# Modulation chunks of the attention in the rooms of x and of the early operand, on ScalarE's DMA queue

## The chip, the cores and the metric

One core of a Trainium2 chip runs the whole program. Its engines are TensorE (PE; PEld is its weight load), VectorE (DVE), ScalarE (ACT), GpSimd (POOL) and SyncE (SP), which here only issues DMAs. The metric is the device time of one execution in microseconds. The kernel before took 772.94 us as the median of three runs (772.45 to 775.13).

## The reference

A trunk of two layers on 256 tokens of width 1024, in f32. Layer 0 mixes tokens with dilated windowed attention in three groups and 16 heads, layer 1 with gated linear attention; each is followed by a gated ConvFFN. Every sub-layer reads a normed input that is scaled and shifted by a modulation vector, which comes from the condition `c`:

```python
for i in range(DEPTH):
    mod = jax.nn.silu(c) @ w_ada[i] + b_ada[i]            # 1024 x 6144 per layer
    sh1, sc1, g1, sh2, sc2, g2 = jnp.split(mod, 6, axis=-1)
    h = rmsnorm(x, norm_mix[i]) * (1.0 + sc1) + sh1
    y = dilated_mixture(h, ...) if i == 0 else gla_mixer(h, ...)
    x = x + g1 * y
    h = rmsnorm(x, norm_ffn[i]) * (1.0 + sc2) + sh2
    x = x + g2 * conv_ffn(h, ...)
return rmsnorm(x, norm_final)
```

`dilated_mixture` computes for each head and group `softmax(q k^T + bias) v` within a causal window, mixes the three groups by their log sums, and multiplies by `w_out`.

## The kernel before

Everything is kept transposed, channels on the 128 partitions and the 256 tokens along the row. A product in f32 is made of three passes with split operands, hi times hi, lo times hi and hi times lo (`mm3`, L197 to L199). So each weight tile goes through three steps, in `split`: SP loads it into a buffer `raw` (1 MB for 2048 columns, L181), ACT casts it to `whi` in two halves (L187), and DVE subtracts to get `wlo` in two halves (L191). There are four `raw` buffers and three pairs of whi and wlo.

The modulation is computed beside the rest, in 48 chunks of 1 MB. `ada_chunk(l, n)` (L151) loads a chunk of `w_ada` with SP into **one of the same four `raw` buffers** (L155), and makes with DVE two products with a sum along the row (L160, into `dot`), each turned by ACT into a column of `mod` (L168, L170). Eight chunks are done in the opening. The other 40 stand in the list `rest`, and `next_ada` takes the next one wherever it is called. 18 of them fall into the attention.

The attention goes through the 16 heads in eight pairs. The turn u of the loop computes for pair u the q and k of three groups (`queries`, each with one wqk tile of 2048 columns: 48 matmuls), then v (`values`, two wv tiles of 1536 columns, into pv[0] and pv[1]), then the scores, and the outputs of the pair before: `turn` transposes the normed probabilities `pn` into `t` (L520), ACT copies `t` to `pt` (L521), `outputs` multiplies `pt` with `v` into `po` (L528, L532) and ACT and DVE make ohi and olo of it (L537, L538). `evacuate` copies q with ACT and k with DVE out of the accumulators (L548, L549), and `by_group` copies v with ACT (L563 to L566). `maxima` and `probabilities` add the bias, take the maximum on DVE (L489), the exponential on ACT (L502) and scale on DVE (L508, L509). Pair 7's outputs are computed between the matmuls of the projection (`project`, accumulators `py`), which follows the attention.

`x_all` holds x. At first it holds it with its tokens in the order of their residues, which the attention's norm reads in the opening. In the turn u = 2, SP loads x in its own order into it (L692), for the residual behind the attention (L327). `early_x` are eight tiles of 272 columns that hold an operand of the ConvFFN's first products; column 256 of each takes a shift (`shift_columns`, L286), the others a scaled x (L292).

The order of the instructions on each engine is set by a scheduler that simulates a time line, under the constraints that `behind(...)` and `issue_after` set. Each engine works through its own list in order, SP's DMA issues too: what stands behind a waiting instruction waits as well.

Of the kernel before, what the change touches and what calls it, by code (L numbers as in the profile page):

```python
# [11 lines left out]
F32 = mybir.dt.float32  # L12
# [6 lines left out]
P = 128  # L19
D = 1024  # L20
T = 256
KT = D // P
# [35 lines left out]
def trunk(ctx: ExitStack, tc: tile.TileContext, I, out):  # L58
    nc = tc.nc
# [3 lines left out]
    state = ctx.enter_context(tc.tile_pool(name="state", bufs=1))  # L63
# [8 lines left out]
    def bank(name="ps", tag=None):  # L72
        tag = tag or next(cycle)
        return psum.tile([P, 512], F32, tag=tag, name=name, bufs={"p": 2, "s": 4, "t": 2}[tag])
# [11 lines left out]
    x_all = state.tile([P, KT, T], F32, name="x_all")  # L86
# [12 lines left out]
    def col(at):  # L99
        return small[:, at : at + 1]  # L100
# [19 lines left out]
    @contextmanager  # L120
    def behind(*those):

        with ExitStack() as st:
            for i in those:
                st.enter_context(tc.issue_after(i.ins))
            yield
# [24 lines left out]
    def ada_chunk(l, n, dmas=1):  # L151
        raw = wraw.tile([P, 2048], F32, tag="raw", name="ada_raw")
        for i in range(dmas):
            c = slice(2048 * i // dmas, 2048 * (i + 1) // dmas)
            nc.sync.dma_start(raw[:, c], I["w_ada"][l, n][:, c])  # L155
        for s in range(2):
            piece, kt = ADA_ORDER[2 * n + s]
            dot = tmp.tile([P, 1], F32, tag="dot", name="dot", bufs=4)
            w = raw[:, D * s : D * s + D]
            last_dot[0] = nc.vector.tensor_tensor_reduce(  # L160
                w, w, c_bc, op0=ALU.mult, op1=ALU.add, scale=1.0, scalar=0.0, accum_out=dot,
            )
            m = state.tile([P, 1], F32, tag=f"mod{l}{piece}{kt}", name="mod")
            b = col(C_BADA + 48 * l + 8 * piece + kt)
            if piece in (1, 4):
                g = col((C_NMIX if piece == 1 else C_NFFN) + 8 * l + kt)
                b1 = (16 if piece == 4 else 0) + 8 * l + kt
                last = nc.scalar.activation(m, dot, AF.Identity, scale=g, bias=one_b[:, b1 : b1 + 1])  # L168
            else:
                last = nc.scalar.activation(m, dot, AF.Identity, bias=b)  # L170
            mod[l, piece, kt] = m
        return last


    last_load, copied, last_lo = [None], [None], [None]
# [101 lines left out]
        chain[kt] = chain[7] = i, j  # L277
        return h_hi[kt], h_lo[kt]

    early_x = [state.tile([P, T + 16], F32, tag=f"ex{k}", name="early_x") for k in range(KT)]  # L280
    last_x, last_sum = [None, None], []

    def shift_columns(l, sub):
# [97 lines left out]
    on_act = [norm_ops[1]]  # L381
# [71 lines left out]
    rest = [(0, n) for n in range(8, 24)] + [(1, n) for n in range(24)]  # L453

    def next_ada():
        if rest:
            ada_chunk(*rest.pop(0))


    heads = [slice(E * hh, E * hh + E) for hh in range(2)]  # L460

    def scores(q, k):
# [52 lines left out]
    def turn(tiles, normed_p, pt):  # L515
        for i in tiles:
            t = bank("t", "ttss"[i])
            for j in range(3):
                c = slice(P * j, P * j + P)
                last = nc.tensor.transpose(t[:, c], normed_p[i][:, c], ident)  # L520
            pt_copy[0] = nc.scalar.copy(pt[:, i, :], t[:, 0:KEYS])  # L521
        return last
# [20 lines left out]
    def evacuate(q, k, g, pq, pk):  # L543

        if g:
            i = nc.scalar.mul(q[g], pq, 0.125)  # L548
            return i, nc.vector.tensor_copy(k[g], pk)  # L549
        qh, ql = q[0]  # L550
        pk = in_order(pk)
        kh, kl = (as_tokens(z[:, 0:T]) for z in k[0])
        nc.scalar.mul(qh, pq, 0.125)
        i = nc.scalar.copy(kh, pk)
        nc.vector.scalar_tensor_tensor(ql, pq, 0.125, qh.bitcast(F32), op0=ALU.mult, op1=ALU.subtract)
        return i, nc.vector.tensor_tensor(kl, pk, kh.bitcast(F32), op=ALU.subtract)
# [11 lines left out]
    def new_qk():  # L568
        q = [[att.tile([P, T], F32R, tag=f"q0{i}", name="q") for i in range(2)]]
        k = [[att.tile([P, T + 2], F32R, tag=f"k0{i}", name="k") for i in range(2)]]  # L570
        for z in k[0]:
            nc.gpsimd.memset(z[:, T:].bitcast(F32), 0.0)
        for g in (1, 2):
            q.append(att.tile([P, T], F32, tag=f"q{g}", name="q"))
            k.append(att.tile([P, T], F32, tag=f"k{g}", name="k"))
        return q, k

    def values(u, half, pv, after=(), low=()):
        with behind(*chain[7]):
            w = split(I["wv"][u - 1, half], 1536, after=(after, after), low=low, late=low)  # L580
        for k4 in range(4):
            kt = 4 * half + k4
            wv = parts(w, 384 * k4, 384)
            for t in range(2):
                ht = [y[:, P * t : P * t + P] for y in h[kt]]
                end = mm3(pv[t][:, :384], ht, wv, kt == 0, kt == KT - 1)
        return end

    def queries(u, g, *qk):
        pq, pk, middle, end = raw_queries(u, g, after=pt_copy[:1] if (u, g) == (3, 0) else ())  # L590
        kept[:] = evacuate(*qk, g, pq, pk)
        with behind(kept[1]):
            next_ada()
        return middle, end

    def raw_queries(u, g, tag="p", low=(), by_parts=False, after=()):
        w = split(I["wqk"][u - 2, g], 2048, low=low, late=low, after=(after, after))
        pqk = bank("pqk", tag)
        pq, pk = pqk[:, :T], pqk[:, T:]
        if by_parts:  # L600
            for part in range(3):
                for kt in range(KT):
                    for i, ps in enumerate((pq, pk)):
                        at = 2 * P * kt + P * i
                        end = mm(ps, w[part == 2][:, at : at + P], h[kt][part == 1], start=(part == kt == i == 0),
                                 stop=(part == 2 and kt == KT - 1 and i == 1))
            return pq, pk, None, end
        for kt in range(KT):
            s, e = kt == 0, kt == KT - 1
            mm3(pq, parts(w, 2 * P * kt), h[kt], s, False)  # L610
            end = mm3(pk, parts(w, 2 * P * kt + P), h[kt], False, e)
            if kt == 3:
                middle = end
        return pq, pk, middle, end

    def by_groups(pv):
        v = [att.tile([P, NG * P], F32, tag=f"v{t}", name="v") for t in range(2)]
        for n in range(2):
            by_group(v[n], pv[n])
        return v  # L620

    def bias_of(u):
        with tc.issue_after(last_load[0].ins):
            return load_bias(u)
# [45 lines left out]
        values(1, 0, pv, low=left[-1][1:])  # L670
    end = values(1, 1, pv, after=left[-1][:1], low=evacuated[1:])
    with behind(evacuated[1]):
        next_ada()
    v = by_groups(pv)
    before = probabilities(*maxima(s, bias))
    bias1 = bias_of(1)
# [4 lines left out]
    for u in range(2, NPAIR):  # L681
        if u > 2:
            bias = bias_of(u)
            qk = new_qk()
        with behind(last):
            if u > 2:
                queries(u, 0, *qk)
            middle, end = queries(u, 1, *qk)
        if u == 2:
            bias = bias_of(u)  # L690
            with tc.issue_after(last_load[0].ins):
                nc.sync.dma_start(x_all, I["xT"])  # L692
        with behind(middle):
            turn((0, 1), *before)
        with behind(end):
            turned = turn((2, 3), *before)
        first = pt_copy[:1] if u == 2 else ()
        if u == 2:
            turned_pt, before = before[1], probabilities(*raised)
        middle, end = queries(u, 2, *qk)  # L700
        if u == 2:
            with behind(end):
                outputs(0, v0, turned_pt)
                turn((0, 1), *before)
        second = pt_copy[:1] if u == 2 else ()
        pv = [bank("pv", "p") for _ in range(2)]
        end = values(u, 0, pv, after=first)
        if u == 2:
            with behind(end):
                turned = turn((2, 3), *before)  # L710
        if u < NPAIR - 1:
            end = values(u, 1, pv, after=second)
        with behind(end, turned):
            s, last = scores(*qk)
        with behind(last):
            last = outputs(u - 1, v, before[1])
        if u == NPAIR - 1:
            with behind(last):
                values(u, 1, pv, low=kept[1:])
        v = by_groups(pv)  # L720
        before = probabilities(*maxima(s, bias))
# [222 lines left out]
    for n in range(4):  # L944
# [7 lines left out]
        for i in range(2):  # L952
            kt = 2 * n + i
# [146 lines left out]
    for n in range(4):  # L1100
# [7 lines left out]
        for et in range(2):  # L1108
            i = 2 * n + et
# [156 lines left out]
```

## Time and profile before

| what | us |
|---|---|
| median of three runs | 772.94 |
| the profiled execution | 769.98 |
| its span in the profile | 768.2 |
| opening, to the first q copied by ACT | 58.1 |
| attention, turns u = 2 to 7, to the last po | 267 |

The granted clock of TensorE was 0.999 in the mean. A row of the timeline has the start, the duration, the engine, the line and the operation; in brackets is the idle time of the engine just before it, and what ended it. A row with x3 stands for several equal instructions in a row. Matmuls overlap: one that is shown with 0.28 us is followed by the next after 0.11. "q1 hardware_dynamic" in the page's list of queues is what SP and ACT issue; over the span the DMA engines were busy with it for 67.4%:

```profile
q1 hardware_dynamic: 36032, 184.84, 67.4%
HBM read 184.17 MB, written 1.10 MB: 241 GB/s over the span
```

### The profile page before, as it was taken

Reading aid. Unit: us, or ns where it says so; the run is one execution under the profiler, and the core shown is the slowest. Engines: PE = TensorE matmul, PEld = TensorE weight load, DVE = VectorE, ACT = ScalarE, POOL = GpSimd, SP = SyncE. Lnnn points to the kernel's source line nnn. Section 1 sums busy time; section 2 is a strip of 40 time slices with the busy share of each in tenths; the row PEclk is TensorE's granted clock in tenths of the full one; section 3 lists DMA queues with packets and bytes.
Section 4 is the critical chain, followed back from the end, with each engine's and each line's share of the span. In section 5 each row is a group of like instructions: output and inputs, shape, how many; then the busy total and the mean of one; then the engine's idle time right before and its main releaser. Section 6 shows DMA issues by size and latency. Waiting matters only on the chain.

```text
span 768.2 us, 15928 instructions
## 1 busy us (share of the span) xinstructions
PE 756.4 (98%) x6420; PEld 730.1 (95%) x6420; DVE 625.2 (81%) x1120; ACT 490.3 (64%) x964; POOL 12.3 (2%) x36
## 2 busy tenths in 40 slices
PE   9999999999999999999999999999999999999997
PEld 5999989999998999999999998898999999999997
DVE  6988886878878788999988868887567998899662
ACT  5566675665666578676766456736667766666552
POOL 0000000000000010000000000000010000000100
PEclk9999999999999999999999999999999999999999
DMA  9989778587787856876656976776254756565741
GB/s 346 388 307 334 255 297 292 200 331 251 276 309 253 297 200 233 279 232 230 221 184 228 334 254 241 289 274 226 79 191 165 232 207 210 177 203 206 259 153 55
DMA packets 36487, 186.29 MB, mean 243 GB/s; under 512 B 8444, under 2 KB 11004, under 8 KB 20286
## 3 DMA queue, kind: packets, MB, share of 16 engines
q1 hardware_dynamic: 36032, 184.84, 67.4%
q8 instruction: 50, 0.82, 0.4%
q10 hardware_dynamic: 382, 0.45, 0.2%
q14 instruction: 23, 0.19, 0.1%
HBM read 184.17 MB, written 1.10 MB: 241 GB/s over the span
## 4 chain that ended last, share of the span: by engine, by line
PE 68%; DMA 13%; DVE 13%; ACT 3%; issue 2%; SPq 0%; ACTq 0%; DVEq 0%
PE pab L199 10%; PE pab L197 10%; PE pab L198 10%; DMA raw<-in_wqk 6%; PE pd L197 5%; PE pd L199 5%; PE pd L198 5%; DVE wlo L191 5%; DMA ada_raw<-in_w_ada 4%; DMA raw<-in_wv 3%; DVE ada_raw L160 3%; PE py L197 2%; PE py L198 2%; PE py L199 2%; PE pv L197 2%
## 5 line engine op out<-in xcount | busy, mean ns | idle before, releaser
L191 DVE TENSOR_TENSOR wlo<-raw,whi 128x1024 fp32r<-128x1024 f32 (+2 forms) x258 | 273.3, 1093 | 60.0 <-ACT whi L187 58.9
L187 ACT CAST whi<-raw 128x1024 fp32r<-128x1024 f32 (+2 forms) x258 | 230.5, 942 | 116.3 <-PE pab L198 40.7
L199 PE MATMUL pab<-hhi,wlo 128*128 128x256 f32 x672 | 184.7, 276 | 0.0
L198 PE MATMUL pab<-hlo,whi 128*128 128x256 f32 x672 | 184.6, 276 | 0.0
L197 PE MATMUL pab<-hhi,whi 128*128 128x256 f32 x672 | 183.2, 277 | 0.0
L198 PEld LDWEIGHTS pab<-hlo,whi 128*128 128x128 f32 x672 | 126.0, 188 | 0.2
L199 PEld LDWEIGHTS pab<-hhi,wlo 128*128 128x128 f32 x672 | 126.2, 188 | 0.0
L197 PEld LDWEIGHTS pab<-hhi,whi 128*128 128x128 f32 x672 | 125.1, 188 | 0.1
L160 DVE CUSTOM_DVE_ANT_0 ada_raw<-ada_raw,c_bc 128x1024 f32<-128x1024 f32 x96 | 113.5, 1221 | 10.3 <-DMA ada_raw<-in_w_ada 10.2
L199 PE MATMUL pd<-ghi,wlo 128*128 128x256 f32 x352 | 97.1, 276 | 0.0
L198 PE MATMUL pd<-glo,whi 128*128 128x256 f32 x352 | 97.1, 276 | 0.0
L197 PE MATMUL pd<-ghi,whi 128*128 128x256 f32 x352 | 96.8, 276 | 0.0
L197 PE MATMUL pqk<-hhi,whi 128*128 128x256 f32 x328 | 92.3, 281 | 0.1
L199 PE MATMUL pqk<-hhi,wlo 128*128 128x256 f32 x328 | 91.3, 278 | 0.0
L198 PE MATMUL pqk<-hlo,whi 128*128 128x256 f32 x328 | 91.0, 277 | 0.0
L199 PEld LDWEIGHTS pd<-ghi,wlo 128*128 128x128 f32 x352 | 66.1, 188 | 0.0
L198 PEld LDWEIGHTS pd<-glo,whi 128*128 128x128 f32 x352 | 66.1, 188 | 0.0
L197 PEld LDWEIGHTS pd<-ghi,whi 128*128 128x128 f32 x352 | 65.9, 188 | 0.0
L197 PEld LDWEIGHTS pqk<-hhi,whi 128*128 128x128 f32 x328 | 61.7, 188 | 0.7 <-issue 0.3
L199 PEld LDWEIGHTS pqk<-hhi,wlo 128*128 128x128 f32 x328 | 61.7, 188 | 0.3 <-issue 0.3
L198 PEld LDWEIGHTS pqk<-hlo,whi 128*128 128x128 f32 x328 | 61.7, 188 | 0.0
L827 ACT ACTIVATE r<-pab,small 128x256 f32<-128x256 f32 x86 | 46.7, 559 | 15.5 <-DVE r L830 15.4
(226 smaller groups left out, 1385.2 us busy)
## 6 DMA issues: line engine op xcount, KB each, us to landing
ada_raw<-in_w_ada SPq DMA_DIRECT2D x46, 1024.0 KB, 5.8
raw<-in_w_up SPq DMA_DIRECT2D x42, 1024.0 KB, 4.9
raw<-in_w_down SPq DMA_DIRECT2D x32, 704.0 KB, 5.2
raw<-in_wqk SPq DMA_DIRECT2D x18, 1024.0 KB, 7.7
raw<-in_wv SPq DMA_DIRECT2D x14, 768.0 KB, 4.6
raw<-in_w SPq DMA_DIRECT2D x6, 960.0 KB, 5.8
raw<-in_w_out_a SPq DMA_DIRECT2D x4, 1024.0 KB, 7.2
raw<-in_w_v_b SPq DMA_DIRECT2D x4, 1024.0 KB, 5.0
```

Of the source, the lines that this page charges most:

```text
L160: last_dot[0] = nc.vector.tensor_tensor_reduce(w, w, c_bc, op0=ALU.mult, op1=ALU.add, scale=1.0, scalar=0.0, accum_out=dot,)
L187: copied[0] = nc.scalar.copy(hi[:, c], raw[:, c])
L191: last_lo[0] = nc.vector.tensor_tensor(lo[:, c], raw[:, c], hi[:, c].bitcast(F32), op=ALU.subtract)
L197: mm(ps, a[0], b[0], start=start, stop=False)
L198: mm(ps, a[0], b[1], start=False, stop=False)
L199: return mm(ps, a[1], b[0], start=False, stop=stop)
L827: nc.scalar.activation(r, u[:, :T], AF.Identity, scale=cw[2], bias=col(C_CB + 44 * l + f))
```

## The change

The 18 chunks of the attention no longer use `raw` and SP's queue. The eight tiles `early_x` become one tile `early_all` of 8 times 272 columns. The first 2048 columns of `early_all` and all of `x_all` are two *rooms*. `room_load(i)` loads chunk i into room i % 2, issued by ACT. The first two are issued behind ACT's last cast of the opening's weights `w0` (`on_act[0]`). `room_ada` stands where `next_ada` stood in the attention: it computes the chunk in its room, and behind it on ACT loads the chunk after the next into the same room; behind the last chunk of room 1 it loads x in its own order into `x_all`. SP's load of it in the turn u = 2 is gone. The chunks after the attention stay as they were.

```diff
@@ ada_chunk
             nc.sync.dma_start(raw[:, c], I["w_ada"][l, n][:, c])
+        return modulation(raw, l, n)
+
+    def modulation(raw, l, n):
         for s in range(2):
             piece, kt = ADA_ORDER[2 * n + s]
...
-    early_x = [state.tile([P, T + 16], F32, tag=f"ex{k}", name="early_x") for k in range(KT)]
+    early_all = state.tile([P, KT, T + 16], F32, name="early_x")
+    early_x = [early_all[:, kt, :] for kt in range(KT)]
...
+    rooms = [z.rearrange("p k t -> p (k t)")[:, 0:2048] for z in (early_all, x_all)]
+    here = rest[:18]
+    del rest[:18]
+
+    def room_load(i):
+        l, n = here[i]
+        nc.scalar.dma_start(rooms[i % 2], I["w_ada"][l, n])
+
+    with behind(on_act[0]):
+        for i in range(2):
+            room_load(i)
+    called = iter(range(len(here)))
+
+    def room_ada():
+        i = next(called)
+        with behind(modulation(rooms[i % 2], *here[i])):
+            if i + 2 < len(here):
+                room_load(i + 2)
+            elif i % 2:
+                nc.scalar.dma_start(x_all, I["xT"])
@@ queries, and once behind pair 1's values
-            next_ada()
+            room_ada()
@@ turn u = 2
-            with tc.issue_after(last_load[0].ins):
-                nc.sync.dma_start(x_all, I["xT"])
```

The scheduler then orders the attention anew. Behind it, the order is the same but for the buffers. In the rows below, a row has the line, the operation, and out<-in with its size; the lines of the changed kernel are higher by 3 to 25.

**Place 1: ACT in the turn u = 2**, from the casts of wqk for groups 1 and 2 on. `prob` are the exponentials of pair 0 (384 columns, then 386), `v<-pv` the copies of pair 1's v, of which the first four empty pv[0]. Before:

```order
L187 CAST whi<-raw 128x1024 x2
L170 ACTIVATE mod<-dot,small 128x1 x2
L502 ACTIVATE prob,m<-prob,m 128x384 x2
L563 COPY v<-pv 64x256
L564 COPY v<-pv 64x2x128
L565 COPY v<-pv 64x128
L566 COPY v<-pv 64x128
```

Now:

```order
L527 ACTIVATE prob,m<-prob,m 128x384 x2
L190 CAST whi<-raw 128x1024 x2
L173 ACTIVATE mod<-dot,small 128x1
L190 CAST whi<-raw 128x1024 x2
L173 ACTIVATE mod<-dot,small 128x1
L470 DMA early_x<-in_w_ada 128x2048
L527 ACTIVATE prob,m<-prob,m 128x386 x2
L588 COPY v<-pv 64x256
L589 COPY v<-pv 64x2x128
L590 COPY v<-pv 64x128
L591 COPY v<-pv 64x128
```

The second pair of casts, a room load and the second pair of exponentials have moved ahead of v.

**Place 2: q and k of group 2.** On DVE in the turn u = 6 (a middle pair), from the k of group 1 on; ISA rows are a chunk's two products. Before:

```order
L549 COPY k<-pqk 128x256
L160 ISA ada_raw,dot<-ada_raw,c_bc 128x1024
L160 ISA dot 128x1
L160 ISA ada_raw,dot<-ada_raw,c_bc 128x1024
L160 ISA dot 128x1
L191 TENSOR_TENSOR wlo<-raw,whi 128x768 x2
L549 COPY k<-pqk 128x256
```

Now:

```order
L574 COPY k<-pqk 128x256
L163 ISA x_all,dot<-x_all,c_bc 128x1024
L163 ISA dot 128x1
L163 ISA x_all,dot<-x_all,c_bc 128x1024
L163 ISA dot 128x1
L194 TENSOR_TENSOR wlo<-raw,whi 128x1024 x2
L574 COPY k<-pqk 128x256
```

What stands ahead of group 2's k is no longer the wlo of this pair's second wv tile but that of the next pair's first wqk tile. On ACT in the last pair, u = 7, from the q of group 1 on, before:

```order
L548 ACTIVATE q<-pqk 128x256
L521 COPY pt<-t 128x384
L170 ACTIVATE mod<-dot,small 128x1
L521 COPY pt<-t 128x384 x3
L187 CAST whi<-raw 128x768 x2
L170 ACTIVATE mod<-dot,small 128x1
L168 ACTIVATE mod<-dot,one_b,small 128x1
L548 ACTIVATE q<-pqk 128x256
L187 CAST whi<-raw 128x1024 x2
```

Now:

```order
L573 ACTIVATE q<-pqk 128x256
L546 COPY pt<-t 128x384
L173 ACTIVATE mod<-dot,small 128x1
L470 DMA x_all<-in_w_ada 128x2048
L546 COPY pt<-t 128x384 x3
L173 ACTIVATE mod<-dot,small 128x1
L290 COPY early_x<-mod 128x1 x3
L171 ACTIVATE mod<-dot,one_b,small 128x1
L290 COPY early_x<-mod 128x1 x4
L190 CAST whi<-raw 128x1024 x2
L573 ACTIVATE q<-pqk 128x256
```

The cast of the second wv tile has gone ahead of these rows, and that of w_out's first tile now stands in front of group 2's q. The shifts into early_x, which stood here and there from u = 3 on, now follow that room's last chunk. The load of x in its own order stands on ACT four rows behind this q.

**Place 3: PE at the last outputs**, between the matmuls of the projection. `t` are the transposes of pair 7, three for each of four tiles. Before:

```order
L520 MATMUL t<-ident,pn 128x128 x3
L199 MATMUL py<-ohi,wlo 128x256
L520 MATMUL t<-ident,pn 128x128 x3
L197 MATMUL py<-ohi,whi 128x256
L520 MATMUL t<-ident,pn 128x128 x3
L198 MATMUL py<-olo,whi 128x256
L199 MATMUL py<-ohi,wlo 128x256
L197 MATMUL py<-ohi,whi 128x256
L198 MATMUL py<-olo,whi 128x256
L199 MATMUL py<-ohi,wlo 128x256
```

After these rows come three more py matmuls, and then po. Now:

```order
L545 MATMUL t<-ident,pn 128x128 x3
L201 MATMUL py<-olo,whi 128x256
L202 MATMUL py<-ohi,wlo 128x256
L545 MATMUL t<-ident,pn 128x128 x3
L200 MATMUL py<-ohi,whi 128x256
L201 MATMUL py<-olo,whi 128x256
L202 MATMUL py<-ohi,wlo 128x256
L545 MATMUL t<-ident,pn 128x128 x6
L553 MATMUL po<-pt,v 64x256 x4
L557 MATMUL po<-pt,v 64x64 x8
```

The py matmuls that stood between the last transposes and po now stand ahead of the last transposes.

More of the change, by code (lines that the diff above doesn't have):

```diff
@@ L672, in trunk @@
     with behind(evacuated[1]):
-        next_ada()
+        room_ada()
     v = by_groups(pv)
```

## The prediction

> **What bounds the kernel.** I read the page first: the busy time of each engine, and the chain that ended last. After that the waits of TensorE (PE) in the attention, 20 to 275 us, the part that the change edits.
>
> ```profile
> span 768.2 us, 15928 instructions
> PE 756.4 (98%) x6420; PEld 730.1 (95%) x6420; DVE 625.2 (81%) x1120; ACT 490.3 (64%) x964; POOL 12.3 (2%) x36
> PE 68%; DMA 13%; DVE 13%; ACT 3%; issue 2%; SPq 0%; ACTq 0%; DVEq 0%
> ```
>
> PE is busy for 756.4 of 768.2 us, so all of its idle time is 11.8 us, over the whole program. The chain of work that ended last gives DMA 13% and DVE 13%, but a chain can run through work that PE does not feel: it does not say that 13% can be had. What PE itself lost in the attention is this (who released it, us, times, longest):
>
> ```profile
> PE pv L197 <- DVE k L549: 1.3, 1, 1.3
> PE pv L198 <- DVE wlo L191: 0.9, 2, 0.5
> PE py L197 <- ACT ohi L537: 0.5, 1, 0.5
> PE pv L197 <- ACT whi L187: 0.5, 1, 0.5
> ```
>
> These are 3.2 us. The windows view, with one stretch for each of four head pairs (from the first po matmul of one turn of the loop to that of the next; the columns are length, PE busy, PEld, DVE, ACT, POOL, clock, DMA share, GB/s), shows what recorded idle time leaves out:
>
> ```profile
> 103.44:132.64 29.20, 29.20 (x277) 28.39 (x272) 22.39 (x46) 17.19 (x45) 0.19 (x2) 1.00 0.72 265
> 132.64:161.86 29.22, 29.22 (x278) 28.36 (x272) 23.51 (x47) 18.46 (x43) 0.19 (x2) 1.00 0.70 250
> 161.86:192.46 30.60, 29.98 (x278) 28.59 (x272) 24.39 (x49) 20.05 (x48) 0.19 (x2) 1.00 0.77 281
> 192.46:221.67 29.21, 29.21 (x278) 28.40 (x272) 23.87 (x48) 18.28 (x42) 0.00 (x0) 1.00 0.80 290
> ```
>
> Three pairs take 29.2 us and have no idle PE; the third one (u = 5) takes 1.4 us longer. So what the change can win is about 3.2 us and the 0.8 us of u = 5 that is not recorded as idle: 4 us at the very best. 0.5% of 772.94 is 3.9 us, about what a measurement of this kernel can tell from no change.
>
> **The change part by part.** I sum against the profiled execution, 769.98 us. The median of the runs is 772.94, so 2.96 us are added at the end.
>
> *The late weights of u = 5.* SP's queue holds weights and modulation chunks in one line, on four shared buffers; its waits in the attention show what it pays:
>
> ```profile
> SPq L181 <- DVE wlo L191: 36.6, 10, 11.7
> SPq L181 <- DVE dot L160: 24.2, 7, 5.5
> ```
>
> A weight load (L181) stood 24.2 us behind chunks that DVE had not read. In u = 5 it reaches PE:
>
> ```profile
> 173.79 4.60 SPq L181 DMA_DIRECT2D raw<-in_wv  x2
> 182.78 1.57 ACT L187 CAST whi<-raw 128x768 fp32r<-128x768 f32 x2 [0.80 <-DMA raw<-in_wv]
> ...
> 182.15 0.33 PE L197 MATMUL pv<-whi,hhi 128*128 128x384 f32 x1
> 183.71 0.40 PE L197 MATMUL pv<-whi,hhi 128*128 128x384 f32 x1
> 184.66 0.44 PE L198 MATMUL pv<-wlo,hhi 128*128 128x384 f32 x1 [0.55 <-DVE wlo L191]
> ```
>
> The second wv half reached ACT at 182.78, so wlo was late for the matmul at 184.66. Afterwards the four buffers serve weights alone in the attention, five loads for each pair, and each of these waits for a wlo several splits back: the load is ready before it is wanted. I take -1.4 us (the pair becomes 29.2). Bounds: -1.4, and 0 if loads stay late. What is late next is k of the last group, below.
>
> *k of the last group in the middle pairs.* The order shows that q and k of group 2 now stand behind the casts and wlo of the next weights. After group 2's last matmul come, on ACT, two casts, and on DVE two wlo and k:
>
> ```profile
> 70.35 2.01 ACT L187 CAST whi<-raw 128x1024 fp32r<-128x1024 f32 x2 [3.44 <-DMA raw<-in_wqk]
> ...
> 73.31 2.36 DVE L191 TENSOR_TENSOR wlo<-raw,whi 128x1024 fp32r<-128x1024 f32 x2
> ```
>
> The first cast half takes 1.0, two wlo 2.36, k 0.42 (the row of 243.99 below): k is there 3.8 us after group 2. PE has 24 matmuls of pv[0] to do first; from 182.15 to 183.71 nine of them start, 0.173 each, so 4.15 us. The cover is 0.35 us: cost 0, and past that every late microsecond is paid in each of four pairs.
>
> *The last pair.* Here only 12 matmuls stand between (2.08 us).
>
> ```profile
> 241.65 1.57 ACT L187 CAST whi<-raw 128x768 fp32r<-128x768 f32 x2 [0.86 <-DMA raw<-in_wv]
> 243.60 0.36 ACT L548 ACTIVATE q<-pqk 128x256 f32<-128x256 f32 x1
> ...
> 243.99 0.42 DVE L549 COPY k<-pqk 128x256 f32<-128x256 f32 x1 [1.43 <-ACT q L548]
> ...
> 244.47 0.44 PE L197 MATMUL pv<-whi,hhi 128*128 128x384 f32 x1 [1.29 <-DVE k L549]
> ```
>
> Before, ACT sat in front of the late cast, q came at 243.60, k at 243.99, and PE lost 1.29. Afterwards the cast ahead of q is that of w_out, whose weights are there, but it waits for group 2's end, since it takes that group's buffer: 2.0 + 0.36 + 0.42 = 2.8 us against 2.08, so about 0.7 us of PE's wait stays. Gain -0.6; bounds -1.3 (no wait) and +0.5 (a wlo or a chunk's reduction of 1.2 us ahead of k).
>
> *The tail.* Before, eight py matmuls lie between the last transposes and po; afterwards none.
>
> ```profile
> 265.62 0.55 PE L520 MATMUL t<-ident,pn 128*128 128x128 f32 x3
> 267.01 1.08 PE L528 MATMUL po<-pt,v 128*64 128x256 f32 x8
> 269.04 0.51 PE L197 MATMUL py<-ohi,whi 128*128 128x256 f32 x2 [0.48 <-ACT ohi L537]
> ...
> 264.57 2.11 ACT L521 COPY pt<-t 128x384 f32<-128x384 f32 x4 [1.27 <-PE t L520]
> ```
>
> The last transposes end at 266.17, the four pt copies at 266.68 and po starts 0.3 later, so the distance is some 0.8 us, which PE now waits for: +0.7, bounds 0 and +1.1. The 0.48 before py stays.
>
> *The opening.* Two of the 1 MB room loads go out on ACT's queue at about 53.6 (behind the last cast of w0, ahead of ACT's row of 53.55), beside the wv load that ACT waits for:
>
> ```profile
> 50.09 0.33 SPq L181 DMA_DIRECT2D raw<-in_wv  x1
> 53.55 2.00 ACT L187 CAST whi<-raw 128x1024 fp32r<-128x1024 f32 x2
> 56.05 1.57 ACT L187 CAST whi<-raw 128x768 fp32r<-128x768 f32 x2 [0.50 <-DMA raw<-in_wv]
> 58.12 0.66 ACT L548 ACTIVATE q<-pqk 128x256 f32<-128x256 f32 x2 [0.50 <-PE pqk L644]
> 59.45 1.22 PE L605 MATMUL pqk<-hhi,whi 128*128 128x256 f32 x9
> ```
>
> Behind this cast are q and k of pair 0, and the raw_queries matmuls from 59.45 on take the bank that pair 0's first k is copied from. ACT had 0.5 us of air ahead of q at 58.12 (it waited for PE), and from q's two halves and k's copy to 59.45 I count another 0.5. The wv load came in just ahead of 56.05, so it still had 2.4 us to go at 53.6. If the rooms take half the engines from it, 2.4 us are added and PE loses 1.4; if it keeps its place, nothing. I take a delay of 1.3 and a loss of +0.3; bounds 0 and +1.5.
>
> By the Trainium skill, "DMA: Bandwidth & Descriptors", section "Queues, rings and completion order", each engine takes packets in turn from the queues that have work. That would give the upper of the two bounds; no run here has yet shown a load on ACT's queue beside one of SP's.
>
> *v behind the casts in u = 2.* After the change ACT does two casts of wqk, a chunk's mod, an issue and the second pair of exps before it copies v; before, v came first:
>
> ```profile
> 74.85 0.37 ACT L563 COPY v<-pv 64x256 f32<-64x256 f32 x1
> 76.17 0.37 ACT L563 COPY v<-pv 64x256 f32<-64x256 f32 x1
> 77.36 0.62 ACT L502 ACTIVATE prob<-prob,m 128x386 f32<-128x386 f32 x1
> ...
> 76.80 0.38 PE L197 MATMUL pqk<-hhi,whi 128*128 128x256 f32 x1
> ```
>
> PE takes up pv[0]'s bank with group 1 of u = 2 at 76.8, and needs the first four v copies for that (74.85 to 76.17, 1.3 us). Afterwards, worked on from the cast of 70.35 quoted above: the first exps end near 70, cast 2.0 (72.0), the chunk's first reduction and mod (72.7), cast 2.0 (74.7), mod and issue (75.4), two exps of 0.6 (76.6), v[0] 1.3: 77.9. So +1.1; bounds 0 (wqk lands early and DVE is earlier) and +2.
>
> *The rest.*
>
> ```profile
> 1.68 0.44 ACTq L94 DMA_DIRECT2D tab<-in_rel_bias  x1
> ...
> ada_raw<-in_w_ada SPq DMA_DIRECT2D x46, 1024.0 KB, 5.8
> ...
> x_all<-in_xT SPq DMA_DIRECT2D x1, 1024.0 KB, 8.0
> ```
>
> ACT gets 19 issues; at 0.44 us (one of its four issues in the opening) that is 8 us over the attention, where in a pair ACT is busy for 17 to 20 of 29 us: hidden, and counted above where an issue stands ahead of something. If that cover were gone, each would cost its 0.44. SP loses 18 chunk loads and xT, which costs and gains nothing beyond the earlier weights. Two waits in u = 2 (the one for whi, and one of the two for wlo) keep their order, a cast behind pt: they stay. A room's load goes out two chunks ahead of its use, and a chunk's load takes 5.8 us, against 29.2 / 3 = 9.7 us from one chunk to the next on the mean: hidden; a late one would hold up DVE's reduction and what stands behind it there, which is rival (b). xT is issued on ACT behind the last pair's q of group 2 and half a cast, so near 248, lands 8.0 later near 256, and its first reader follows the py of 269.04: hidden, by 13 us.
>
> Sum: -1.4 - 0.6 + 0.7 + 0.3 + 1.1 = +0.1: 770.1 for a profiled run, **773.0** beside the median.
>
> **Rivals.**
> (a) *The change doesn't do what it says: the loads are no earlier.* The same bytes go through the same 16 engines, u = 5 and the last pair keep their waits, and only the losses come: +0.7 + 0.3 + 1.1 = +2.1, 775.0. Against it: in u = 5 the DMA share is 0.77, so the engines were not full; SP waited for DVE to free buffers, and the rooms are two more buffers. Chance 0.2. The Trainium skill has this case as a rule, on the same page, section "Issuing engines are not separate DMA queues": issuing from several engines saves only the time of issuing. The waits of SP above speak against its being the limit here, since they are waits for buffers.
> (b) *Slower:* group 2's k comes late in each middle pair. The place is ACT's casts of the next wqk ahead of q, the point is 4.15 us after group 2. A chunk's reduction (1.2 us) that gets ahead of wlo would bring 3.8 to 5.0: 0.85 us in four pairs and 1.2 more in the last one, +4.6 on the sum: 777.6. For it: 0.35 us is little; against it: DVE is busy for 24 of 29 us and its chunk stands ahead of that wlo with its operand loaded well before. Chance 0.15.
> (c) *Faster:* all 4 us go, and the opening and the tail cost nothing: 769.0. For it: DVE and ACT have air. Against it: the casts at 96 to 98 are untouched, and the order itself puts pt right before po. Chance 0.08.
>
> **How the numbers follow.** The forecast has 0.57. Its own bounds run from -1.4 - 1.3 = -2.7 (770.2) to about +3.5 when two of the losses are at their upper end (776.4). The range takes in (a) and most of (b): 769.6 to 777.4. Faster by over 0.5% (below 769.1): half of (c) and a little, 0.07. Slower by over 0.5% (above 776.8): (b), and 0.04 of upper ends of the others, 0.19. Same: 0.74.
>
> **What would show it.** Right: the stretch of u = 5 at 29.2 us; no wait of ACT's cast for wv there; PE's wait for k in the last pair at 0.7; a wait of PE for v near 77 and for pt before the last po. Wrong: a wait of PE for k in the pairs u = 3 to 6, which is (b); SP still waiting for DVE with wv late, which is (a). The prediction fails as a whole if the layers behind the attention change by a microsecond or more: I count nothing there.

## The result, and the profile after

The changed kernel takes **777.39 us** (median of 14 runs, 774.58 to 779.91); in the same runs the kernel before takes 772.30 us (median of 14, 769.21 to 775.13). The ratio is 1.0066, with a 95% interval of 1.0050 to 1.0082: slower by 0.7%, 5.1 us. The predicted time was 773.0, the range 769.6 to 777.4. The profiled execution took 778.79 us, of which 777.0 are the span; it is one of the longer ones of the changed kernel, where that of the kernel before (769.98) was one of the shorter ones.

The page of the changed kernel, its busy times and the shares of the chain that ended last:

```profile
span 777.0 us, 15933 instructions
PE 760.2 (98%) x6420; PEld 734.9 (95%) x6420; DVE 625.5 (81%) x1120; ACT 492.5 (63%) x964; POOL 12.1 (2%) x36
PE 86%; DVE 6%; DMA 5%; issue 1%; ACT 1%; SPq 0%; ACTq 0%; DVEq 0%
```

Two things stand out here. PE idles 16.8 us (777.0 - 760.2) where it idled 11.8. And PE is *busy* 3.8 us longer with the same 6420 matmuls: some of them were slower. A comparison of waits alone sees only the first. In the page's list of queues q1 fell from 184.84 to 164.91 MB and q10 grew from 0.45 to 20.37 MB, the room loads and x: so q10 is ACT's queue, and q1 is SP's alone and not what both issue, as was said further up.

PE's waits in the attention, 20 to 290 us, in the columns of the list before (who released it, us, times, longest):

```profile
PE pqk L200 <- ACT v L591: 5.1, 1, 5.1
PE pv L200 <- DVE k L574: 0.7, 1, 0.7
PE po L553 <- ACT pt L546: 0.6, 1, 0.6
PE py L200 <- DVE m L514: 0.5, 1, 0.5
...
PE pv L201 <- DVE wlo L194: 0.4, 1, 0.4
```

The wait for k fell from 1.3 to 0.7, one of the two waits for wlo is gone, and the wait for pt is new; the prediction has all three (0.7 left for k, the 0.55 of u = 5 gone, 0.7 for pt). The wait for DVE's m is new as well and stands in no term. New and large is the first row: PE waits 5.1 us, once, for ACT's copy of v. The four middle pairs, in the windows view with the columns of before:

```profile
110.85:140.06 29.21, 29.21 (x279) 28.40 (x273) 24.32 (x49) 19.72 (x45) 0.19 (x2) 1.00 0.83 296
140.06:169.27 29.21, 29.21 (x278) 28.40 (x273) 24.06 (x49) 18.89 (x42) 0.19 (x2) 1.00 0.81 281
169.27:198.47 29.20, 29.20 (x278) 28.39 (x272) 24.07 (x49) 19.10 (x44) 0.19 (x2) 1.00 0.81 284
198.47:227.69 29.22, 29.22 (x280) 28.41 (x273) 24.04 (x49) 18.68 (x43) 0.00 (x0) 1.00 0.81 286
```

All four take 29.2 us now: u = 5 has lost its 1.4. But the first of them begins at 110.85, where it began at 103.44: 7.4 us were lost ahead of it. Around that place, ACT from the end of pair 0's work to the copies of v in u = 2 (start, us, what it ran; in brackets its idle time before and who ended it):

```profile
73.49 2.00 ACT L190 CAST whi<-raw 128x1024 fp32r<-128x1024 f32 x2 [3.65 <-DMA raw<-in_wqk]
...
76.05 1.99 ACT L190 CAST whi<-raw 128x1024 fp32r<-128x1024 f32 x2 [0.36 <-PE s L495]
...
81.43 0.26 ACT L591 COPY v<-pv 64x128 f32<-64x128 f32 x1
```

and PE there, with the clock granted to it, in stretches of 2 us (the clock is the number behind POOL's):

```profile
75.96 0.69 PE L502 MATMUL s<-k,q 64*64 64x64 f32 x32
81.74 0.58 PE L200 MATMUL pqk<-hhi,whi 128*128 128x256 f32 x1 [5.08 <-ACT v L591]
82.12 0.41 PE L201 MATMUL pqk<-hlo,whi 128*128 128x256 f32 x1
82.34 0.41 PE L202 MATMUL pqk<-hhi,wlo 128*128 128x256 f32 x1
...
80.00:82.00 2.00, 0.26 (x1) 0.26 (x2) 1.79 (x7) 1.94 (x7) 0.00 (x0) 0.56 0.81 284
82.00:84.00 2.00, 2.00 (x10) 2.00 (x11) 1.97 (x10) 1.03 (x5) 0.00 (x0) 0.50 0.98 394
84.00:86.00 2.00, 2.00 (x12) 2.00 (x11) 0.17 (x1) 2.00 (x7) 0.00 (x0) 0.50 1.04 433
86.00:88.00 2.00, 2.00 (x15) 2.00 (x15) 0.00 (x0) 0.44 (x2) 0.00 (x0) 0.73 0.99 418
88.00:90.00 2.00, 2.00 (x20) 2.00 (x19) 0.00 (x0) 0.01 (x1) 0.00 (x0) 1.00 1.03 434
```

The scores of pair 1 end at 76.65; the first product of group 1 starts at 81.74. From about 80.2 to 87.1 the clock is 0.5 on the mean of these stretches, and the products start 0.22 us apart (82.12, 82.34); at 1.0, from 88 to 90, twenty recorded ones start in 2 us, 0.1 apart. So from 81.74 to 87.1, 5.3 us, PE does work of half that time: **the wait costs 5.1 and the slow clock behind it about 2.5** (measured from the first of these products to the first transpose, 8.05 us against 5.57 before). That is the busy time that grew.

Why the cast is late is read from SP's queue. Its rows, its longest wait for a room, from the DMA view the load in question (issues, KB each, us from issue to landing), and a stretch of the windows ahead of wqk's issue (its last two numbers are the DMA share and GB/s):

```profile
63.10 0.60 SPq L357 DMA_DIRECT2D bias<-rows_d  x1
...
67.69 1.82 SPq L184 DMA_DIRECT2D raw<-in_wqk  x2
...
SPq L357 <- DMA x_all<-in_w_ada: 3.4, 1, 3.4
x_all<-in_w_ada ACTq DMA_DIRECT2D x1, 1024.0 KB, 11.9
...
64.00:66.00 2.00, 2.00 (x25) 1.73 (x28) 1.23 (x2) 0.01 (x1) 0.00 (x0) 1.00 0.35 86
```

The load into the second room (x_all) was issued by ACT at 51.21 and took 11.9 us, to 63.1. An issue of a bias on SP waited 3.4 us for exactly this landing, and the wqk loads stand behind it: issued at 67.69, where they were issued at 65.16 before. The data are there at 73.49 instead of 70.35. Of these 3.1 us 2.5 are the later issue; the load itself took 5.8 us where it had taken 5.2. The DMA engines were not full ahead of it: their share is 0.35 from 64 to 66.

### The profile page after: what moved, and what is told of

It reads as the page before. It is cut to its first block, busy times and chain, and to the rows that moved or that the text cites. A ratio compares the mean times of both kernels' runs of the same rounds, so it can differ in the third digit from the quotient of the medians.

```text
span 777.0 us, 15933 instructions
## 1 busy us (share of the span) xinstructions
PE 760.2 (98%) x6420; PEld 734.9 (95%) x6420; DVE 625.5 (81%) x1120; ACT 492.5 (63%) x964; POOL 12.1 (2%) x36
## 3 DMA queue, kind: packets, MB, share of 16 engines
q1 hardware_dynamic: 33296, 164.91, 60.1%
q10 hardware_dynamic: 3118, 20.37, 7.2%
## 4 chain that ended last, share of the span: by engine, by line
PE 86%; DVE 6%; DMA 5%; issue 1%; ACT 1%; SPq 0%; ACTq 0%; DVEq 0%
PE pab L201 10%; PE pab L202 10%; PE pab L200 10%; PE pd L201 5%; PE pd L200 5%; PE pd L202 5%; PE pqk L200 5%; PE pqk L202 5%; PE pqk L201 5%; PE pv L201 3%; PE pv L202 3%; PE pv L200 3%; PE py L200 2%; PE py L201 2%; PE py L202 2%; DMA ada_raw<-in_w_ada 2%
## 5 line engine op out<-in xcount | busy, mean ns | idle before, releaser
L163 DVE CUSTOM_DVE_ANT_0 ada_raw<-ada_raw,c_bc 128x1024 f32<-128x1024 f32 x60 | 70.9, 1219 | 10.2 <-DMA ada_raw<-in_w_ada 10.1
```

The source lines that it names most:

```text
L163: last_dot[0] = nc.vector.tensor_tensor_reduce(w, w, c_bc, op0=ALU.mult, op1=ALU.add, scale=1.0, scalar=0.0, accum_out=dot,)
```

## The experiments

Theories for the 5.1 + 2.5 us. *Order*: v stands behind ACT's casts. *Late issue*: wqk is issued late, since SP waits behind the room's load. *Traffic*: the 2 MB of the first two rooms (1 MB each) go through the 16 engines ahead of wqk, whenever SP issues it. *Idle clock*: part of the loss is no wait at all but the clock after it. The kernel before ran beside each on the same chip: 772.06 us (21 runs) beside the first four, 773.11 (24 runs) beside the last four. Beside the changed kernel it took 772.30, so a difference of about 1 us between medians of different groups says nothing. Line numbers of the experiments are their own, up to four off.

**v first.** The casts of the third group of wqk in u = 2 wait for v:

```
-        ... after=pt_copy[:1] if (u, g) == (3, 0) else ())
+        ... after=pt_copy[:1] if (u, g) == (3, 0) else v_copy[:1] if (u, g) == (2, 2) else ())
```

(v_copy holds the last copy of the latest v.)

> One constraint is added to the changed kernel: ACT's casts of wqk for group 2 of u = 2 come behind the copies of pair 1's v. Theory Q (the loss is one wait in u = 2: v is copied behind two casts, of which the first waits for a late weight load): PE's wait for v there falls from 5.1 us to under 1, the clock stays at 1.0 from 80 to 88 us, and the time falls by about 7 us against the changed kernel's 777.4, to 770 to 771 (ratio to the kernel before 0.997 to 0.999). Rival S (the loss is spread: room loads and weight loads take bandwidth from each other, k and po come later in every pair): at most 1 us less, 776.

Measured: 778.37 us, ratio 1.0079 (1.0050 to 1.0108), and PE's wait for v is still 4.7. The order did change: only one of the two casts is left ahead of v. ACT's timeline shows what took its place:

```profile
78.10 0.33 ACTq L470 DMA_DIRECT2D early_x<-in_w_ada  x1
78.48 0.62 ACT L527 ACTIVATE prob<-prob,m 128x386 f32<-128x386 f32 x1 [3.93 <-DMA bias<-rows_d]
...
79.70 0.35 ACT L590 COPY v<-pv 64x256 f32<-64x256 f32 x1
```

ACT now stands for 3.9 us at the *issue* of the next room's load, which waits for a bias transfer of SP's queue to land (the profile shows the wait at the exps, the next work of ACT); exps and v stand behind the issue. I had expected 770 to 771: a miss for "order" alone. With the order mended, this issue alone still holds v back.

**Rooms late.** The first two loads of rooms go out behind pair 0's v, at 60.70 and 61.96 instead of 50.8 and 51.2:

```
-    with behind(on_act[0]):
-        for i in range(2):
-            room_load(i)
...
     with behind(left[-1][0], left[-3][0]):
         v0 = by_groups(pv)
+    with behind(v_copy[0]):
+        for i in range(2):
+            room_load(i)
```

> The first two room loads go out behind ACT's copies of pair 0's v, near 63 us, instead of at 51; nothing else is edited. Theory L (the cast was late because SP's bias loads and the wqk load behind them stood in line until the second room load had landed at 63): the wqk load of group 1 of u = 2 is issued before 65 us instead of 67.7, its cast starts at 70 or before instead of 73.5, PE's wait for v is at most 1.5 us, and the time is 770 to 773. Rival O (the order of ACT alone makes the wait, whatever the load does): 4 us or more of the wait stay, 775 or more.

Measured: 773.92 us, ratio 1.0030 (1.0005 to 1.0056). ACT's timeline for the cast, the issue of its load on SP, and PE's wait for v:

```profile
73.40 1.05 ACT L190 CAST whi<-raw 128x1024 fp32r<-128x1024 f32 x1 [7.62 <-DMA raw<-in_wqk]
...
62.96 1.10 SPq L184 DMA_DIRECT2D raw<-in_wqk  x2
...
PE pqk L200 <- ACT v L590: 4.4, 1, 4.4
```

wqk is issued at 62.96, 2.2 us *earlier* than in the kernel before, and is there at 73.40 all the same, 10.4 us later (the two loads of that row took a median of 11.3). The wait and the time that I had expected were missed. An early issue alone is not enough: here the loads of both rooms go out right ahead of wqk and share the engines with it, which are full (a share of 1.00 from 62.96 to 73.40). So this run shows "traffic" for its own order of loads. It doesn't show it for the changed kernel, where the second room had landed at 63.1, before wqk was issued. The wait stays at 4.4, the clock falls behind it as before. The median is 3.5 us below that of the changed kernel. In the profiles 1.4 of them are won up to the first po of u = 2 (95.25 for 96.65): 0.7 of the wait and 0.9 in the opening, less 0.2 of slow clock. The rest can't be assigned from one profile of each.

**Rooms on SP.** The same loads, x's reload too, issued by SP's queue again, into the same two rooms:

```
-        nc.scalar.dma_start(rooms[i % 2], I["w_ada"][l, n])
+        nc.sync.dma_start(rooms[i % 2], I["w_ada"][l, n])
```

> The rooms stay, but their loads and that of x are issued by SP, behind the same instructions as in the changed kernel. Theory B (what takes the wait out of u = 5 is that the chunks have buffers of their own): u = 5 takes 29.2 us as in the changed kernel, not 30.6, and the second queue is not needed for it; time 769 to 773, as far as SP's line is not held up by a load that waits for its room. Rival A (it is the second queue): u = 5 is back at 30 us or more, and weight loads wait for DVE's dot behind the room loads; 774 to 778.

Measured: 774.84 us, ratio 1.0040 (1.0014 to 1.0066). The windows view of u = 5, SP's wait at the rooms, PE's wait for v and a stretch behind it:

```profile
166.51:195.72 29.21, 29.21 (x279) 28.40 (x272) 24.12 (x49) 19.12 (x44) 0.19 (x2) 1.00 0.83 287
...
SPq L470 <- DVE dot L163: 32.2, 14, 2.5
PE pqk L200 <- ACT v L591: 2.7, 1, 2.7
...
82.00:84.00 2.00, 2.00 (x20) 2.00 (x19) 0.60 (x5) 1.73 (x7) 0.00 (x0) 1.00 0.22 44
```

u = 5 keeps its gain although SP issues everything and waits 32.2 us in all for rooms to be read. So the gain comes from the two added buffers, not from the second queue. That agrees with the Trainium skill, "DMA: Bandwidth & Descriptors", section "Issuing engines are not separate DMA queues", by which loads of all issuing engines share the same 16 engines and interleave. The time, though, lies above the 769 to 773 that I had expected with this theory. The wait for v is 2.7 here, and in this execution the clock stays at 1.0 (the mean granted clocks of the ten runs are 0.995 to 1.0): 5.76 us from the first product of group 1 to the first transpose, 2.3 less than in the changed kernel. The opening is dearer: the products that start at 59.24 in the changed kernel start at 61.19.

**Idle PE, filled.** The changed kernel with matmuls that nobody reads (ones by ones) between pair 1's scores and group 1, so that PE doesn't idle:

```
     raised = maxima(s, bias1)
+    ps = bank("warm", "t")
+    with behind(last):
+        for i in range(40):
+            last = mm(ps[:, :P], ones_d, ones_d, start=True, stop=True)
```

> PE gets 40 matmuls of 128x128 on constants between the scores of pair 1 and group 1 of u = 2, where it waited 5.1 us in the changed kernel; nothing reads them. Theory I (idle time of PE lowers its clock afterwards): PE is busy with them for some 4.4 us, the wait that is left is about 1 us, the granted clock from 82 to 87 us is 1.0 instead of 0.5, group 1 takes 5.5 us instead of 8, and the time is some 2.4 us below the changed kernel, 775. Rival P (the clock falls there for another reason, such as the load on DVE, ACT and the DMAs): the clock is 0.5 there all the same, 777 to 778.

Measured: 777.52 us, ratio 1.0078 (1.0047 to 1.0110): nothing won. Each of the 40 shows as two matmuls of 0.11 us, so the filler took 9.0 us in place of the 4.4 that I had meant, and held PE some 2.7 us past the end of the copies. Behind it the clock is 1.0, and the piece to the first transpose takes 5.54 us. The clock term moved as expected, the size of the filler hid it; so once more with 20:

> The filler of the run before again, with half as many matmuls (20 lines, 4.5 us of PE where 40 took 8.9 and ran past the wait by 2.7). Theory I (PE's idle time lowers its clock afterwards): group 1 of u = 2 starts when v has been copied, some 5.3 us after the scores, and takes 5.5 us to the transposes as before the change, not 8.05; time 2.5 us below the changed kernel, 775. Rival P (the clock falls for another reason): 8 us, 777.

Measured: 774.91 us, ratio 1.0021 (1.0006 to 1.0036), 2.5 us below the changed kernel's median; against the kernel before beside each, +1.8 us in place of +5.1. PE's timeline, and a stretch of the windows:

```profile
76.08 4.73 PE L708 MATMUL warm<-ones_d 128*128 128x128 f32 x40
82.49 0.39 PE L200 MATMUL pqk<-hhi,whi 128*128 128x256 f32 x1 [1.68 <-ACT v L591]
82.72 0.28 PE L201 MATMUL pqk<-hlo,whi 128*128 128x256 f32 x1
82.83 0.28 PE L202 MATMUL pqk<-hhi,wlo 128*128 128x256 f32 x1
...
84.00:86.00 2.00, 2.00 (x19) 2.00 (x18) 0.71 (x5) 1.33 (x5) 0.00 (x0) 1.00 1.02 424
```

The copies of v are no earlier (the first product starts at 82.49), but the products now start 0.11 apart at clock 1.0, 5.76 us to the first transpose. "Idle clock" holds: about 2.5 us of the loss are paid after the wait, by work that would have been at full clock. It isn't one execution's accident: the mean granted clock is 0.998 to 1.0 in all ten runs here, and 0.993 to 0.996 in all 14 of the changed kernel.

**v first, and the issue behind v.** The first run's edit, and the issue that stood in front of v there goes behind pair 1's copies of v:

```
-            if i + 2 < len(here):
+            if 0 < i < len(here) - 2:
                 room_load(i + 2)
+            elif i == 0:
+                pass
...
     v = by_groups(pv)
+    with behind(v_copy[0]):
+        room_load(2)
```

> On top of the run with v ahead of the second cast, the load of chunk 2 into room 0 is issued by ACT behind the copies of v instead of ahead of them. Theory H (that load's issue waits on ACT for a bias load of SP's queue to land, 3.9 us in that run, and v's copies stand behind it): PE's wait for v falls from 4.7 us to 1.5 at most, the clock stays at 1.0, time 769 to 772. Rival W (v is late because the first cast of wqk is late, at 72 to 73): the wait stays at 3 us or more.

Measured: 773.48 us, ratio 0.9998 (0.9984 to 1.0011). The wait fell from 4.7 to 1.9, a little over the 1.5 that I had allowed, since the cast still starts at 73.39; the time is above the 769 to 772 that I had expected. So the issue was what stood ahead of v. SP's issue of wqk, and PE's timeline, which shows a surprise:

```profile
67.36 1.73 SPq L184 DMA_DIRECT2D raw<-in_wqk  x2
...
78.21 0.39 PE L200 MATMUL pqk<-hhi,whi 128*128 128x256 f32 x1 [1.94 <-ACT v L595]
78.43 0.28 PE L201 MATMUL pqk<-hlo,whi 128*128 128x256 f32 x1
...
79.52 0.42 PE L200 MATMUL pqk<-hhi,whi 128*128 128x256 f32 x1
```

PE resumes at full clock (the first products start 0.22 and then 0.12 apart, 0.28 long), falls to half at 79.1 (0.42 long), 0.9 us *into* the work, and is back at 82.5. This cost 1.6 us (7.19 against 5.57 to the first transpose). Of the 7.6 us in the changed kernel some 3.6 are left (1.9 of wait, 1.6 of clock), and they hang on the late cast.

**Room 1 late as well.** The run above, and the first load of the second room goes out behind pair 1's v too, at 74.69 in place of 51.2. So only 1 MB of rooms stands ahead of wqk:

```
     with behind(on_act[0]):
-        for i in range(2):
-            room_load(i)
+        room_load(0)
...
     with behind(v_copy[0]):
+        room_load(1)
         room_load(2)
```

> On top of that, the first load of room 1 also goes out behind the copies of v, near 77 us instead of 51; its chunk is read at 92. Theory C (in the opening the two rooms bring 1 MB more ahead of the wqk load than the kernel before had, which at about 400 GB/s is 2.6 us; this made the cast late): the cast of wqk for group 1 starts at 70.5 or before, PE's wait for v is below 0.5 us, the first po of u = 2 is at 89 to 89.5 as in the kernel before, time 769.5 to 771.5 with what u = 5 and the last pair gained and the tail lost. Rival: the cast stays at 72 or later, and time does not differ from the run before.

Measured: **769.06 us**, ratio **0.9953** (0.9936 to 0.9970), faster than both kernels and a little below the 769.5 to 771.5 that I had expected. SP's issue of wqk, ACT's timeline and PE's:

```profile
64.10 1.01 SPq L184 DMA_DIRECT2D raw<-in_wqk  x2
...
70.18 2.00 ACT L190 CAST whi<-raw 128x1024 fp32r<-128x1024 f32 x2 [4.48 <-DMA raw<-in_wqk]
...
73.67 0.35 ACT L591 COPY v<-pv 64x256 f32<-64x256 f32 x1
...
75.48 0.38 PE L200 MATMUL pqk<-hhi,whi 128*128 128x256 f32 x1
```

The cast starts at 70.18 (70.35 in the kernel before), v is copied from 73.67 on, and the first product follows the scores at once, at clock 1.0. Against the last run only that room's load was moved, so the 3.2 us by which the cast is earlier are the price of its megabyte in the opening. SP's rows show by which way it was paid: wqk is issued 3.3 us earlier than in the last run (64.10 for 67.36) and takes as long from there to the cast, 6.1 us for 6.0. So in the changed kernel "late issue" is the way: SP no longer stands behind that room's landing. The median falls by 4.4 us, of which the wait and the slow clock that are gone make 3.6. That it is below the kernel before has its reason in the terms that stay: u = 5 and the last pair, -2.0, against +0.8 in the tail; beyond that its opening came 1.3 us earlier in the one profile, of which u = 2 gives back 0.4; I explain neither.

**The tail as well.** The run above, with twelve py matmuls of the projection (its second tile, two of the eight steps in the sum) put behind the last transposes, so that PE has work while ACT copies pt:

```
-            turn((2, 3), *before)
-        elif (n, kt) == (1, 3):
+            turned_last[0] = turn((2, 3), *before)
+        elif (n, kt) == (1, 6):
...
-                with behind(*(ends[n - 2 :][:1] if (n, kt) == (2, 2) else ())):
+                with behind(*(ends[n - 2 :][:1] if (n, kt) == (2, 2) else turned_last if between and n == 1 and kt in (5, 6) else ())):
```

> On top of that, 12 of the py matmuls of the projection are held behind the last transposes, so that po has cover again. Theory T (po waited for pt because nothing stood between): PE's wait of 0.6 us for pt before the last po goes, and with it 0.5 to 0.8 us of the time; 768.8 to 771. Rival: pn comes too late for the earlier transposes, which then wait, and nothing is won.

Measured: **767.20 us**, ratio **0.9923** (0.9907 to 0.9938). PE's timeline there:

```profile
261.45 1.48 PE L546 MATMUL t<-ident,pn 128*128 128x128 f32 x12
262.68 0.37 PE L200 MATMUL py<-ohi,whi 128*128 128x256 f32 x1
...
264.23 1.08 PE L554 MATMUL po<-pt,v 128*64 128x256 f32 x8
```

po starts without a wait, and from the last turn's po to the end of the tail 18.8 us pass in place of 19.5. So 0.7 us of the step from 769.06 to 767.20 are shown by the profiles. The medians differ by 1.9, the intervals overlap by a little, and more than the 0.7 isn't claimed. This is the fastest version of the study: the idea of the change, without the loss at its opening and its tail.

## Why the prediction was right and wrong

The time lies at the upper edge of the range, but the likeliest case, "same" at 773.0, is not what happened. It was slower by 0.7%, which had a chance of 0.19, and for a reason that no rival named. That the range still holds it is luck: its upper end was drawn for rival (b), which did not happen. By the steps:

- **The late weights of u = 5**, -1.4: the pair takes 29.2 instead of 30.6. Right, and rooms on SP show that the buffers do it. Rival (a), no earlier loads, is out.
- **k of the last group in the middle pairs**, 0: right. The list of waits has none there, all four pairs take 29.2. That rival (b) comes to 777.6 and the measurement to 777.4 is an accident.
- **The last pair**, -0.6: PE's wait for k is 0.7 of 1.3, and the stretch is shorter by 0.63. Right.
- **The tail**, +0.7: the wait for pt is 0.6. Beside it stands 0.5 us that I hadn't counted: a py matmul waits for DVE's m, since a chunk's reduction and a wlo went ahead of that m on DVE (from 256.03 to 259.45 in its timeline). The stretch is longer by 1.19.
- **The opening**, +0.3: the products that were to start 0.3 late start at 59.24, where they started at 59.45. I had put both issues of rooms at 53.6; ACT issued them at 50.8 and 51.2, ahead of its last cast of w0, not behind it. And wv was ready by 55.0, 5.9 us after its issue at 49.08, as in the kernel before (50.09 to 56.05): the loss of half the engines, on which the upper bound was built, didn't reach it. The price of these loads was paid a pair later.
- **v behind the casts in u = 2**, +1.1, bounds 0 and +2: **this is the step that failed**. It measured 5.1 of wait and 2.5 of slow clock, 7.6 in all. The order on ACT was foreseen, and its steps were right in length: from the cast to the end of the second cast 4.4 us were forecast (70.35 to 74.7), 4.5 came; from there to the first v 1.9 forecast, 2.4 came. Two other things were wrong. The chain was started from the *old* landing of wqk, 70.35, although 2 MB now went out ahead of it in the opening, where the kernel before had one chunk (issued at 57.31). SP's line waited for the second of them, wqk was issued 2.5 us later and landed 3.1 us later; with that load moved behind v its cast is back at 70.18. And the sum had no term for the clock after a long wait, which the filler prices at 2.5 us.

The terms as they came out in the attention: -1.4 - 0.6 + 1.2 + 7.4 = +6.6 us (7.4 for everything up to the first po of u = 2). The profiled executions differ by 8.8; the 2.2 that are left lie behind the attention, 503.4 us for 501.2. The prediction named a change there of a microsecond or more as a sign that it fails as a whole, and these executions have one. The windows show what most of it is:

```profile
534.00:536.00 2.00, 2.00 (x11) 2.00 (x12) 2.00 (x2) 2.00 (x4) 0.00 (x0) 0.55 0.54 106
```

The clock is at half again, for 3.4 us (0.55 here, 0.59 from 536 to 538), with PE at work: 1.7 us lost. Two other profiled executions have the same near 534 and 530 (v first; v first and the issue behind v) and take 503.9 and 502.8 us for that part. The remaining experiments don't have it and take 500.6 to 501.8. So it is the clock and not work that was added behind the attention; how often an execution of either kernel meets this fall isn't known. That 6.6 is still above the 5.1 between the medians isn't settled; the interval of the ratio reaches 6.3.

## What to carry to other kernels

When a change moves transfers to an earlier place, every later landing in the trace of before is out of date: begin each chain behind it with what now lies ahead of it, the bytes and the issues that wait for them, not with the old time of arrival. Put loads that are needed late behind the work that is urgent, and issue nothing on a computing engine in front of work that another engine waits for. And price a wait of PE of several us at more than its length: here half as much again was lost to the clock behind it.

## What the runs showed of the hardware

**The clock after idle time.** Waits of 5.1, 4.7 and 4.4 us (the changed kernel, v first, rooms late) were followed by a clock of 0.5 for 6.8 us each, worked out from the mean clocks of the 2 us stretches (for the changed kernel 0.56, 0.50, 0.50, 0.73 from 80 to 88: half from 80.2 to 87.1). A wait of 1.9 us was followed by 3.4 us of it, 0.9 us after PE had resumed. Waits of 2.7 us (rooms on SP) and 1.7 us (filler of 20) weren't followed by any. A wait of 0.9 us near 530, which all ten traces have, was followed by 3.4 us of it in three. So the length of the wait doesn't decide alone. Nor does the kernel: of the ten runs with v first and the issue behind v, two have a mean granted clock of 1.0 (770.11 and 771.16 us), the others 0.995 to 0.998 (772.77 to 774.58 us). The Trainium skill, "TensorE: Matmul & The Clock Gate", section "Part 1: The HAM clock gate", has a free-running window of about 3.4 us, with half rate after an idle window. The lengths agree, one and two such windows; if an idle window is one without any work, the wait of 1.9 us doesn't agree, since PE was at work for 1.5 of the 3.4 us that ended with the fall. A window that runs on its own and asks for a share of work would fit these waits, and the differences between runs of one kernel, but that is argued, not shown.

**An issue can wait for another queue's transfer.** SP's issue of a bias stood 3.4 us for a room's load of ACT's queue, and ACT's issue of a room's load 3.9 us for a bias of SP's queue, though neither touches the other's data. On ACT the compute behind the issue stands as well. The traces show the cause: the issues of SP and ACT together take the semaphore (a counter) that tells of their landing from the same eight in turn, and each issue waits until the earlier transfer on its semaphore has landed. The bias that SP issued at 63.10 has the semaphore of the room's load of 51.21, whose last count came at 63.09; the room's load that ACT issued at 78.10 in v first has that of the bias of 69.06, whose last count came at 78.08. So a slow transfer holds up the issue that comes eight later, on whichever engine it stands. More semaphores weren't tried.

**A megabyte beside another queue.** The load of the second room took 11.9 us from issue to landing beside SP's loads, wqk a median of 11.3 beside two rooms. In the kernel before a chunk's load took 5.8 as the median of all, but 9.9 as that of the four issued between 40 and 80 us, where SP issued every load. So loads in this place are slow with one queue too, and what the second queue adds isn't shown.
